# Loading w by row set over all partitions, with two sets of its first quarter in GpSimd's queue

## The chip, the cores and the metric

The kernel runs on one core of one Trainium2 chip. The metric is the device time of one execution in microseconds (us), lower is better. Three runs before the change took 904.36, 904.37 and 904.57 us, median 904.37.

## The reference

x is 16 x 2048 x 1024, w is 1024 x 1024 and decay has 1024 entries, all fp32. The product is followed by a running sum along the sequence that fades by decay at each step:

```
xw = x @ w
out[:, 0] = xw[:, 0]
for t in range(1, S):
    out[:, t] = decay * out[:, t - 1] + xw[:, t]
```

## The kernel before

The 16 x 2048 rows are cut into 64 chunks of 512 rows, and two chunks make a group. A step is one of the eight tiles n (128 columns of w) for one group. TensorE multiplies in bf16 and accumulates over eight tiles k of 128 rows of w. ScalarE (ACT), VectorE (DVE) and GpSimd (POOL) then form the running sum (lines 171 to 254: pairs of neighbours are joined on GpSimd, VectorE scans every second element, GpSimd fills in the others), VectorE transposes the result (line 266), and SP stores it.

x is loaded by `load` (line 105) in GpSimd's queue, cast to bf16 on the way. One load brings a quarter q of x's columns into 32 partitions, for blocks j0 to j1 of 32 rows each. VectorE transposes blocks of 32 x 32 (`turn`, line 115) into `xw`, where two bf16 neighbours stay together as a pair; `part` (line 123) splits the pairs into `xt`. A matmul (line 131) can read either the pairs or `xt`.

The order of all work around the start is written out by hand in `agenda`, letter by letter; `pin` keeps it as the order on each engine and queue. The entry -99 is the start:

```
-99: "M0 U0 M1 M2 M3 U1 U2 w0 W1 w2 W3 K0 K1 K2 K3 E0 E1 G0 E2 G1 E3 F2 G3 W4 w5 W6 W7 D ..."
```

- M0 and M1 are the first and second part of chunk 0, M2 and M3 of chunk 1, four loads each (one for each q). The parts are set by `cuts`: nine and seven blocks for chunk 0, eight and eight for chunk 1.
- w comes in quarters (h, e): h is the half of its columns, e the parity of k. A quarter has four sets m, and k = 2m + e. Quarter (0, 0) is loaded as fp32 in SP's and ACT's queues before the agenda begins, two loads each; U0, U1 and U2 bring (0, 1), (1, 0) and (1, 1) as bf16 in GpSimd's queue. `load_w` (line 307) issues four loads for a quarter, each of them one q in 32 partitions with all four m. The quarters lie in `room`, two output buffers (`ot`) that are not needed yet.
- w0, W1, w2, W3 settle quarter (0, 0): `settle` (line 314) copies one set m into `wsb`, on ScalarE (small letter) or VectorE (capital). W4 to W7 settle (0, 1), W8 to W11 (1, 0), w12 to w15 (1, 1).
- K0 to K3 (line 348) copy one element of each of M0's four loads into a gate; spins, matmuls on zeros (line 332), keep TensorE busy before and behind them.
- E (turn), F and G (part) prepare the parts of chunks 0 and 1, D prepares decay. L loads a quarter of a later chunk.

At step 0 the matmuls of chunks 0 and 1 for n = 0 to 3 run in four parts of 32: chunk 0's first part, even k and then odd k; its second part in the same way; chunk 1's first part; chunk 1's second part. After them step 4 asks for the half h = 1 of w.

GpSimd's loads have eight semaphores in turn. So a load is issued only when the load eight before it in that queue has landed.

Of the kernel before, what the change touches and what calls it, by code (L numbers as in the profile page):

```python
# [10 lines left out]
BF16 = mybir.dt.bfloat16  # L11
# [3 lines left out]
def _ap(ap_obj: bass.AP, new_ap, extra_offset=0):  # L15
    return dataclasses.replace(
        ap_obj,
        ap=[list(p) for p in new_ap],
        offset=ap_obj.offset + extra_offset,
    )  # L20
# [5 lines left out]
def kernel(  # L26
# [26 lines left out]
    nc = tc.nc  # L53
    pin = tc.keep_in_program_order
    B, S, D = x.shape
    assert w.shape == (D, D)

    NQ = 4
    P = 32
    CQ = D // NQ  # L60
    K = CQ // P
    M = K // 2
    TL = 512
    NJ = TL // P
    NC = S // TL
    R = K // 2
    CH = D // 2
# [8 lines left out]
    def ring(pool, name, count, shape, dtype=FP32):  # L76
        i = turns[name] = turns.get(name, -1) + 1
        return pool.tile(shape, dtype, name=f"{name}{i % count}")

    def quad(q):  # L80
        return slice(q * P, (q + 1) * P)
# [12 lines left out]
    def ot_tile(nj):  # L94
        return ring(sb, "ot", 4, [128, nj, CR])
# [3 lines left out]
    xt_of = {}  # L99
# [25 lines left out]
    def matmul(ps, n, k, xt, t0=0, t1=TL, start=0, pairs=None):  # L125
        if pairs is None:
            rhs = xt[:, k // 2, k % 2, t0:t1]
        else:
            rhs = pairs[:, k // 2, t0 // P:t1 // P, :, k % 2].rearrange("p j i -> p (j i)")
        lhs = wsb[:, k, n].rearrange("p q i -> p (q i)")  # L130
        pin(nc.tensor.matmul(  # L131
            out=ps[:, t0:t1] if ps.shape[1] >= t1 else ps,
            lhsT=lhs,
            rhs=rhs,
            start=(k == 0 and t0 == start),
            stop=(k == K - 1),
        ))
# [3 lines left out]
    class Tile:  # L141
# [45 lines left out]
        def copy(self):  # L187
            self.xs = sb.tile([128, 2 * TL], FP32, name=f"xs{self.lot % 3}")[:, 0:self.T]
            size = self.T // len(self.parts())
            for i, ps in enumerate(self.parts()):  # L190
                pin(nc.scalar.copy(out=self.xs[:, i * size:(i + 1) * size], in_=ps))  # L191
# [82 lines left out]
    class Outlet:  # L274
# [8 lines left out]
        def store(self, b, t0):  # L283
# [4 lines left out]
            for j in range(0, self.nj, nj):  # L288
# [8 lines left out]

    room = [ot_tile(2 * NJ).rearrange("p j c -> p (j c)") for _ in range(2)]
    size = M * CH
    stage = {(0, 0): room[0][:, 0:size],  # L300
             (0, 1): room[0][:, size:size * 3 // 2].bitcast(BF16),
             (1, 0): room[1][:, 0:size // 2].bitcast(BF16),
             (1, 1): room[1][:, size // 2:size].bitcast(BF16)}

    def load_w(queues, h, e):
        for i, q in enumerate((0, 2, 1, 3)):
            pin(queues[i % len(queues)].dma_start(  # L307
                out=stage[h, e][quad(q)].rearrange("p (m d) -> p m d", m=M),
                in_=_ap(w, [[2 * D, P], [2 * P * D, M], [1, CH]],
                        (q * CQ + e) * D + h * CH)))  # L310

    def settle(h, e, m, copy):
        src = stage[h, e][:, m * CH:(m + 1) * CH]
        pin(copy(out=wcols[:, 2 * m + e, h],
                 in_=src.rearrange("p (q r i) -> p q r i", q=NQ, r=R)))

    idle = const.tile([128, TL], BF16, name="idle")
    spare = ring(psp, "spare", 1, [128, TL])
    rows = const.tile([128, 2, P], FP32, name="rows")
    touch = const.tile([128, 1], BF16, name="touch")  # L320
    load_w((nc.sync, nc.scalar), 0, 0)
    pin(nc.vector.memset(idle, 0.0))  # L322
    pin(nc.vector.memset(rows, 0.0))
    pin(nc.scalar.copy(out=touch, in_=idle[:, 0:1]))
# [8 lines left out]

    spin(22, idle[:, 0:128])
    H = NJ // 2
    cuts = (((0, H + 1), (H + 1, NJ)), ((0, H), (H, NJ)))
    for q in range(NQ):
        pin(nc.sync.dma_start(
            out=rows[q * P:q * P + R],
            in_=_ap(decay, [[P, R], [CH, 2], [1, P]], q * CR)))  # L340
# [8 lines left out]
        spin(3 if q < NQ - 1 else 1, gates[q])  # L349

    def load_part(i):
        load_w((nc.gpsimd,), *((0, 1), (1, 0), (1, 1))[i])

    def part_one(i, copy):
        part(i // 8, copy, i % 4, i % 4 + 1, *cuts[i // 8][i // 4 % 2])
# [29 lines left out]
    def bank(name, count):  # L385
        return ring(psp, name, count, [128, R, 128])

    def cross(rs, some):
        for i in some:
            for r in rs:  # L390
                t = 2 + i * 128
                pin(nc.tensor.transpose(  # L392
                    out=blocks[i][:, r], in_=tiles[len(slots) - R + r].so[:, t:t + 128], identity=ident))
# [27 lines left out]
    def turn_and_load(c):  # L421
# [38 lines left out]
        "L": lambda i: load(*loads.pop(0)) if loads else None,  # L460
    }
    agenda = {
        -99: "M0 U0 M1 M2 M3 U1 U2 w0 W1 w2 W3 K0 K1 K2 K3 E0 E1 G0 E2 G1 E3 F2 G3 W4 w5 W6 W7 D E4 E5 G4 E6 G5 E7 F6 G7 E8 E9 G8 E10 G9 E11 F10 G11 E12 L E13 G12 L E14 G13 E15 L F14 G15",
        0: "p0 z0 W8 W9 W10 W11",
        1: "g0",
        2: "L S1 L",
# [76 lines left out]
    def rest(s):  # L543
        do = [f"S{s - 1}"] if tiles[s - 1].paired else []
        do.append(f"C{s - 1}")
        if tiles[s - 2].paired:
            do.append(f"B{s - 2}")
        return do + [f"B{s - 1}"] + later.get(s, []) + ["L"] * len(loads)

    def perform(do):  # L550
        for deed in do:
            deeds[deed[0]](int(deed[1:] or 0))
# [3 lines left out]
    for step, (g, n) in enumerate(slots):  # L556
        T = TL * len(g)
        left = step - len(slots)
        if n % R == 0:
            ns, nj = range(n, n + R), T // P  # L560
            if left == -2 * R:
                outlets = [Outlet(ns, H, half) for half in range(2)]
            else:
                pieces = 1 if left < -7 * R else 2 if left < -6 * R else nj // H
                outlets = [Outlet(ns, nj, pieces=pieces)]
        if left == -R:
            outlets = []
        if step == 0:
            heads = [ring(psp, "ps", 3, [128, T]) for _ in range(3)]
            firsts = [ps[:, 0:TL] for ps in heads] + [spares[0]]  # L570
            seconds = [ps[:, TL:T] for ps in heads] + [spares[1]]
            for j0, j1 in cuts[0]:
                for e in range(2):
                    for k in range(e, K, 2):
                        for i in range(R):
                            matmul(firsts[i], i, k, xt_of[0], j0 * P, j1 * P, j0 * P,
                                   pairs=None if e else xw_of[0])
            for k0 in range(0, K, 2):
                for i in range(R):
                    for k in (k0, k0 + 1):  # L580
                        matmul(seconds[i], i, k, xt_of[1], 0, H * P,
                               pairs=xw_of[1] if k0 < 4 else None)
            for i in range(R):
                for k in range(K):
                    matmul(seconds[i], i, k, xt_of[1], H * P, TL, H * P,
                           pairs=xw_of[1] if i < 2 else None)
        if step < R:
            ps = heads[n] if n < 3 else tuple(spares)
        else:
            if step == K + 1:  # L590
                ps = nexts
            elif len(g) == 2 or n % R < 3:
                ps = ring(psp, "ps", 3, [128, T])
            else:
                ps = ring(psp, "spare", 1, [128, TL])
            todo = [(k, l) for k in range(K) for l in range(len(g))]
            if step < K:
                todo.sort(key=lambda kl: kl[0] % 2)
            elif step == K:
                todo = []  # L600
                nexts = (ring(psp, "spare", 1, [128, TL]), ring(psp, "ps", 3, [128, T])[:, TL:T])
                for l in range(len(g)):
                    for i, one in enumerate((ps[:, l * TL:(l + 1) * TL], nexts[l])):
                        for k in range(K):
                            matmul(one, n + i, k, xt_of.get(g[l]),
                                   pairs=xw_of[g[l]] if l or not i and k >= M else None)
            elif step == K + 1:
                todo = []
            if left == -1:
                ps = tuple(both[:, t:t + TL // 2] for t, both in zip(  # L610
                    (0, TL // 2), (ps, ring(psp, "ps", 3, [128, TL]))))
                blocks += [bank("spare1", 1), bank("ps", 3)]
                for t, half in zip((0, TL // 2), ps):
                    for k in range(K):
                        matmul(half, n, k, xt_of[g[0]], t, t + TL // 2, t)
                    if not t:
                        cross((1,), (0, 1))
                todo = []
            for k, l in todo:
                matmul(ps[:, l * TL:(l + 1) * TL], n, k, xt_of[g[l]])  # L620
        tiles.append(Tile(g, n, ps, outlets))
        do = agenda.get(step, agenda.get(left) if left >= -20 else None)
        if do is None:
            do = usual(step)
        else:
            do = do.split()
            if left == -20:
                do = rest(step) + do
        perform(do)
# [29 lines left out]
```

## Time and profile before

| what | value |
|---|---|
| median of three runs | 904.37 us |
| profiled execution | 905.1 us, span 903.3 us |
| TensorE busy | 896.9 us (99%) |
| VectorE busy | 824.2 us (91%) |
| ScalarE busy | 685.9 us (76%) |
| GpSimd busy | 657.1 us (73%) |
| DMA, first 24 us | about 180 to 390 GB/s from 2 us on |

All times in the profile are in us from the start of the span. An idle time stands with the instruction that ends it and with what released that instruction. A load's issue is short; its bytes move later, and it has landed when all the DMA engines that carry it have added to its semaphore. The trace records every packet of the DMA engines with its queue, start and size, and every landing.

### The profile page before, as it was taken

Reading aid. Unit: us, or ns where it says so; the run is one execution under the profiler, and the core shown is the slowest. Engines: PE = TensorE matmul, PEld = TensorE weight load, DVE = VectorE, ACT = ScalarE, POOL = GpSimd, SP = SyncE. Lnnn points to the kernel's source line nnn. Section 1 sums busy time; section 2 is a strip of 40 time slices with the busy share of each in tenths; the row PEclk is TensorE's granted clock in tenths of the full one; section 3 lists DMA queues with packets and bytes.
Section 4 is the critical chain, followed back from the end, with each engine's and each line's share of the span. In section 5 each row is a group of like instructions: output and inputs, shape, how many; then the busy total and the mean of one; then the engine's idle time right before and its main releaser. Section 6 shows DMA issues by size and latency. Waiting matters only on the chain.

```text
span 903.3 us, 12163 instructions
## 1 busy us (share of the span) xinstructions
PE 896.9 (99%) x4216; PEld 412.8 (46%) x4216; DVE 824.2 (91%) x632; ACT 685.9 (76%) x957; POOL 657.1 (73%) x755
## 2 busy tenths in 40 slices
PE   9999999999999999999999999999999999999998
PEld 5444444444444444444444444444444444444444
DVE  4899998998999999999998999999999999999998
ACT  4899867877877877878778778777787787787743
POOL 7978678877767778777677687777777776876632
PEclk9999999999999999999999999999999999999999
DMA  9999999999999999999999999999999999999858
GB/s 193 184 215 215 223 244 208 215 229 232 248 239 251 253 241 246 250 258 249 241 237 226 222 231 226 232 229 227 233 227 226 233 231 222 227 230 214 184 143 232
DMA packets 403182, 204.77 MB, mean 227 GB/s; under 512 B 9392, under 2 KB 402096, under 8 KB 403120
## 3 DMA queue, kind: packets, MB, share of 16 engines
q1 hardware_dynamic: 265808, 134.77, 60.9%
q0 software_dynamic: 137024, 68.70, 56.4%
q8 instruction: 33, 0.54, 0.2%
q10 hardware_dynamic: 288, 0.52, 0.2%
q14 instruction: 29, 0.24, 0.1%
HBM read 138.42 MB, written 134.22 MB: 302 GB/s over the span
## 4 chain that ended last, share of the span: by engine, by line
PE 92%; DMA 3%; DVE 2%; issue 1%; POOL 1%; ACT 0%; DVEq 0%; POOLq 0%; ACTq 0%
PE ps L131 91%; DMA xb<-in_x_dram 2%; POOL xb L105 1%; DMA ot<-in_w_dram 1%; PE spare L131 1%; DVE so L229 1%; DVE ot L266 0%; DVE so L210 0%; DVE xw L115 0%; POOL xs L205 0%; PE spare L392 0%; PE ps L392 0%; ACT h L171 0%; DVE h L401 0%; POOL so L199 0%
## 5 line engine op out<-in xcount | busy, mean ns | idle before, releaser
L131 PE MATMUL ps<-xt,wsb 128*128 128x512 bf16 (+1 forms) x4024 | 865.6, 378 | 0.4 <-DVE so L229 0.4
L131 PEld LDWEIGHTS <-wsb 128*128 128x128 bf16 x4168 | 407.3, 98 | 479.0 <-issue 1.7
L205 POOL TENSOR_TENSOR xs<-h,xs 128x512 f32<-128x512 f32 (+1 forms) x190 | 242.8, 1278 | 183.1 <-ACT h L171 84.6
L266 DVE STREAM_TRANSPOSE ot<-so 128x1024 f32<-128x1024 f32 (+2 forms) x264 | 300.1, 1175 | 5.7 <-DMA out_dram<-ot 3.6
L191 ACT COPY xs<-ps 128x1024 f32<-128x1024 f32 (+1 forms) x190 | 188.8, 994 | 145.2 <-PE ps L131 141.6
L254 POOL TENSOR_TENSOR so<-h,xs 128x512 f32<-128x512 f32 (+1 forms) x190 | 241.1, 1271 | 48.0 <-ACT h L171 28.1
L123 ACT COPY xt<-xw 128x2048 bf16<-128x2048 bf16 (+3 forms) x136 | 242.1, 1788 | 8.9 <-DVE xw L115 8.9
L105 POOL DMA_DIRECT2D xb<-in_x_dram x264 | 174.2, 661 | 6.7 <-DMA xb<-in_x_dram 3.1
L171 ACT ACTIVATE h<-so,dec 128x512 f32<-128x512 f32 (+1 forms) x190 | 145.3, 765 | 37.3 <-DVE so L210 34.0
L115 DVE STREAM_TRANSPOSE xw<-xb 128x2048 f32<-128x2048 f32 (+3 forms) x78 | 147.4, 1902 | 8.8 <-DMA xb<-in_x_dram 8.8
L210 DVE TENSOR_TENSOR_SCAN so<-spare,keep,xs 128x512 f32<-128x512 f32 (+1 forms) x97 | 119.6, 1236 | 24.1 <-POOL xs L205 23.9
L210 DVE TENSOR_TENSOR_SCAN so<-spare,xs 128x512 f32<-128x512 f32 x93 | 113.2, 1219 | 26.4 <-POOL xs L205 23.5
L171 ACT ACTIVATE h<-ps,dec 128x512 f32<-128x512 f32 (+1 forms) x190 | 129.9, 683 | 0.0
L229 DVE TENSOR_TENSOR_SCAN so<-dec,ps 128x1024 f32<-128x1024 f32 x34 | 76.8, 2261 | 1.0 <-ACT h L171 1.0
L229 DVE TENSOR_TENSOR_SCAN so<-dec,keep,ps 128x1024 f32<-128x1024 f32 (+1 forms) x35 | 75.9, 2169 | 0.0
L258 ACT COPY keep<-so 128x1 f32<-128x1 f32 x136 | 25.3, 189 | 9.6 <-DVE so L229 9.0
L201 ACT COPY so<-keep 128x1 f32<-128x1 f32 x97 | 18.4, 191 | 2.7 <-DVE ot L266 2.5
L131 PE MATMUL ps<-xw,wsb 128*128 128x256 bf16 (+3 forms) x72 | 12.3, 306 | 0.4 <-DVE xw L115 0.4
L131 PE MATMUL spare<-xt,wsb 128*128 128x512 bf16 (+3 forms) x60 | 12.6, 330 | 0.0
L199 POOL MEMSET so<- 128x1 f32 x93 | 10.6, 116 | 0.6 <-DVE ot L266 0.6
L332 PE MATMUL spare<-idle 128*128 128x512 bf16 x22 | 7.4, 515 | 1.2 <-DVE idle L322 1.2
L307 POOL DMA_DIRECT2D ot<-in_w_dram x12 | 6.5, 545 | 1.0 <-issue 0.4
(39 smaller groups left out, 37.9 us busy)
## 6 DMA issues: line engine op xcount, KB each, us to landing
out_dram<-ot SPq DMA_DIRECT2D x236, 512.0 KB, 11.1
xb<-in_x_dram POOLq DMA_DIRECT2D x248, 256.0 KB, 7.9
out_dram<-ot SPq DMA_DIRECT2D x56, 128.0 KB, 2.6
out_dram<-ot SPq DMA_DIRECT2D x8, 256.0 KB, 4.0
ot<-in_w_dram POOLq DMA_DIRECT2D x12, 128.0 KB, 6.1
xb<-in_x_dram POOLq DMA_DIRECT2D x8, 128.0 KB, 4.8
out_dram<-xb SPq DMA_DIRECT2D x3, 256.0 KB
xb<-in_x_dram POOLq DMA_DIRECT2D x4, 144.0 KB, 6.2
```

Of the source, the lines that this page charges most:

```text
L105: pin(nc.gpsimd.dma_start(out=xb_of[c][quad(q), j0:j1], in_=_ap(x, [[D, P], [P * D, j1 - j0], [1, CQ]], (b * S + t0 + j0 * P) * D + q * CQ)))
L115: pin(nc.vector.transpose(out=dst.rearrange("p (m j i) -> p j m i", m=M, i=P)[:, j0:j1, m0:m1], in_=src.rearrange("p (j m c) -> p j m c", ...
L123: pin(copy(out=xt_of[c][:, m0:m1, :, j0 * P:j1 * P], in_=src))
L131: pin(nc.tensor.matmul(out=ps[:, t0:t1] if ps.shape[1] >= t1 else ps, lhsT=lhs, rhs=rhs, start=(k == 0 and t0 == start), stop=(k == K - 1),))
L171: pin(nc.scalar.activation(out=h[:, i * size:(i + 1) * size], in_=src, func=mybir.ActivationFunctionType.Copy, scale=dec[:, self.n:self.n ...
L191: pin(nc.scalar.copy(out=self.xs[:, i * size:(i + 1) * size], in_=ps))
L205: pin(nc.gpsimd.tensor_tensor(out=odds, in0=self.g, in1=odds, op=ALU.add))
L210: pin(nc.vector.tensor_tensor_scan(out=so[:, 3:T + 2:2], data0=squares[-1][:, n:n + 1].to_broadcast([128, T // 2]), data1=self.xs[:, 1:T:2 ...
L229: pin(nc.vector.tensor_tensor_scan(out=so[:, t + 2:t + 2 + size], data0=dec[:, n:n + 1].to_broadcast([128, size]), data1=ps, initial=befor ...
L254: pin(nc.gpsimd.tensor_tensor(out=self.so[:, 2:T + 2:2], in0=self.h, in1=self.xs[:, 0:T:2], op=ALU.add))
L258: pin(nc.scalar.copy(out=self.keep, in_=self.so[:, self.T + 1:self.T + 2]))
L266: pin(nc.vector.transpose(out=outlet.ot[:, :, c0:c0 + P], in_=self.so[:, 2 + t0:2 + t0 + nj * P].rearrange("p (i t) -> p i t", t=P)))
```

## The change

A load of w now brings one set m of a quarter for all four q, that is 128 partitions with one row of 512 columns each, instead of one q with four sets. Its source runs over the four quarters q, then 32 rows, then 512 columns. Of quarter (0, 0), set 0 is loaded in SP's queue and set 1 in ACT's, as fp32; sets 2 and 3 come in GpSimd's queue as bf16 and stand there before chunk 0's first part. The units of U are renumbered: U0 is these two sets, U1 to U3 are the other quarters, four loads each. A settle waits for its own set alone. Chunk 0's first part has ten blocks instead of nine, chunk 1's first part seven instead of eight, and the matmuls of chunk 1 take their bound from `cuts`.

```diff
-    stage = {(0, 0): room[0][:, 0:size],
-             (0, 1): room[0][:, size:size * 3 // 2].bitcast(BF16),
+    stage = {(0, 1): room[0][:, size:size * 3 // 2].bitcast(BF16),
...
-    def load_w(queues, h, e):
-        for i, q in enumerate((0, 2, 1, 3)):
-            pin(queues[i % len(queues)].dma_start(
-                out=stage[h, e][quad(q)].rearrange("p (m d) -> p m d", m=M),
-                in_=_ap(w, [[2 * D, P], [2 * P * D, M], [1, CH]],
-                        (q * CQ + e) * D + h * CH)))
+    def spot(h, e, m):
+        if (h, e) == (0, 0):
+            if m < 2:
+                return room[0][:, m * CH:(m + 1) * CH]
+            return room[0][:, 2 * CH:3 * CH].bitcast(BF16)[:, (m - 2) * CH:(m - 1) * CH]
+        return stage[h, e][:, m * CH:(m + 1) * CH]
+
+    def load_w(queue, h, e, m):
+        pin(queue.dma_start(
+            out=spot(h, e, m),
+            in_=_ap(w, [[CQ * D, NQ], [2 * D, P], [1, CH]],
+                    (2 * P * m + e) * D + h * CH)))
...
-    load_w((nc.sync, nc.scalar), 0, 0)
+    load_w(nc.sync, 0, 0, 0)
+    load_w(nc.scalar, 0, 0, 1)
...
-    cuts = (((0, H + 1), (H + 1, NJ)), ((0, H), (H, NJ)))
+    cuts = (((0, H + 2), (H + 2, NJ)), ((0, H - 1), (H - 1, NJ)))
...
     def load_part(i):
-        load_w((nc.gpsimd,), *((0, 1), (1, 0), (1, 1))[i])
+        for m in range(0 if i else 2, M):
+            load_w(nc.gpsimd, i // 2, i % 2, m)
...
-        -99: "M0 U0 M1 M2 M3 U1 U2 w0 W1 w2 W3 ...
+        -99: "U0 M0 U1 M1 M2 M3 U2 U3 w0 W1 w2 W3 ...
...
-                        matmul(seconds[i], i, k, xt_of[1], 0, H * P,
+                        matmul(seconds[i], i, k, xt_of[1], 0, Q,
```

## The prediction

> **What bounds the kernel now.** I read the page first, then the chain of waits for the first 70 us, then the timeline of the first 26 us and around 40 and 68 us, then the trace's packet and landing records of the first 45 us.
>
> The page: TensorE is busy from end to end at full clock, so only its start and its few gaps can be won or lost.
>
> ```profile
> PE 896.9 (99%) x4216; PEld 412.8 (46%) x4216; DVE 824.2 (91%) x632; ACT 685.9 (76%) x957; POOL 657.1 (73%) x755
> PEclk9999999999999999999999999999999999999999
> ```
>
> The chain (start, duration, what) shows that everything up to 68 us hangs on transfers and on who may issue the next one:
>
> ```profile
> 1.31 6.19 DMA xb<-in_x_dram
> ...
> 15.70 6.52 DMA ot<-in_w_dram
> ...
> 28.51 11.19 DMA xb<-in_x_dram
> ...
> 65.62 2.32 DVE so L229
> ...
> 67.98 2.10 PE ps L131 x9
> ```
>
> The timeline (start, duration, engine, line, tile, count, idle time before it and its releaser) has the waits that the change touches:
>
> ```profile
> 6.92 1.14 ACT L314 CAST wsb<-ot 128x512 bf16<-128x512 f32 x2 [3.75 <-DMA ot<-in_w_dram]
> 9.77 1.56 DVE L115 STREAM_TRANSPOSE xw<-xb 128x288 f32<-128x288 f32 x4 [2.05 <-DMA xb<-in_x_dram]
> 10.61 0.55 PE L131 MATMUL ps<-xw,wsb 128*128 128x288 bf16 x3
> 12.45 0.70 DVE L314 COPY wsb<-ot 128x512 bf16<-128x512 bf16 x3 [0.78 <-DMA ot<-in_w_dram]
> 15.31 0.46 PE L131 MATMUL ps<-xw,wsb 128*128 128x224 bf16 x3 [0.38 <-DVE xw L115]
> 22.50 2.03 POOL L105 DMA_DIRECT2D xb<-in_x_dram  x3 [1.53 <-DMA ot<-in_w_dram]
> 39.83 2.31 DVE L115 STREAM_TRANSPOSE xw<-xb 128x2048 f32<-128x2048 f32 x1 [1.38 <-DMA xb<-in_x_dram]
> 67.98 1.24 PE L131 MATMUL ps<-xt,wsb 128*128 128x512 bf16 x5 [0.45 <-DVE so L229]
> ```
>
> To be seen: the first matmul (10.61) waits for chunk 0's first part (last landing 9.64), not for w's first quarter (last landing 6.76). GpSimd's queue is full from 5.2 to 26 us; its loads land one after the other. Its issue of chunk 2 (22.50) waits for the first load of w's third quarter, eight loads earlier (landed 22.22). Chunk 3 lands at 39.70, VectorE takes it at 39.83 and is then busy without a gap, and at 67.98 TensorE waits 0.45 for VectorE. So two things set the end: when TensorE starts, with 0.45 us of slack, and when GpSimd's queue reaches chunk 2, without any.
>
> **The change, part by part.**
>
> Form of w's loads. Before, a load has 32 rows of partitions outermost; after, its source has the four quarters outermost (4, then 32 rows). The only loads of before with four outermost are decay's: each has one landing record at issue and then four more (6.40 to 6.54 for the first), where every other early load has sixteen. So four engines carry such a load in SP's queue, and I take that for the two new ones in SP's and ACT's queues. The Trainium skill, "DMA: Bandwidth & Descriptors", section "Why a DMA increments its semaphore by 16 and not by 1", says that the engine count is the largest number up to 16 that divides the outermost sizes of both sides, and that SP's and ACT's queues use the lowest-numbered engines; it speaks against this change, the trace's decay loads agree in the count, and no run here shows which engines.
>
> Cost of that. Each of the two loads has 128 packets of 2 KB; on four shared engines that is 64 packets each, at 84 ns (their median between 2.2 and 3.8 us) 5.4 us. From the first packet (1.76) this ends at 7.15; decay's 32 small packets behind them on SP's queue, 8 per engine at the 40 ns of the smallest x packets, add about 0.35: 7.5. Spread over all engines it would be 16 packets each, done by 4.0 like the first pair of before, whose end markers ran from 3.3 to 4.0. If the two loads fell on different fours: 32 packets, 4.8.
>
> GpSimd's queue. U0 (two sets, all partitions) now stands ahead of M0. For loads in this queue I know only all sixteen engines. A half-quarter load there takes 0.65 us from landing to landing with 8 packets per engine, 81 ns each; two make 1.3. M0 has 20 packets per engine and load instead of 18, at 40 ns (0.72 per load over 18): four make 3.2. The four slow engines finish M0 at 7.5 + 1.3 + 3.2 = 12.0; with 0.95 from last packet to last landing (before, the late engines ended M0 near 5.6 + 0.2 + 2.9 = 8.7, and it landed at 9.64) M0 lands at 12.9 instead of 9.64. GpSimd issues the first eight loads without a wait, as before, so its two extra issues (0.55 each) lie under this; without that cover they cost 1.1.
>
> TensorE's start. Before: 0.97 after M0's last landing, of which 0.2 was the spins' backlog (the last spin started at 10.39, the transpose was ready at 10.26). After: the spins run dry and wait for the gates, so 0.8 plus the wider transpose (0.04): 13.7.
>
> The four parts, 32 matmuls each. Spacings before: 288 columns 127 and 122 ns (pairs, copies), 224 98, 256 112. Ten blocks (320) 141 and 136: 4.43 us; seven 3.13; nine 4.0. Six (192 columns) have no row: bounded by the 224-column spacing, 98 ns (weight loads take 96 there), 3.1, and by the columns, 84 ns, 2.7. I lean to neither. The Trainium skill, "TensorE: Matmul & The Clock Gate", section "Back-to-back issue gap", has 81 ns sustained for 128 columns, which would make it 2.7; no run here shows it. Sum 14.25 to 14.7 against 14.95 (10.61 to 25.56): settling by set removes the 0.15 at 12.79; and the 0.38 at 15.31 goes, since M1 lands 4.6 after M0 (U1 2.6, four loads of 12 packets per engine 2.0) and is transposed 0.55 later, while the ten blocks end 0.84 + 4.43 = 5.27 after it. Neither stall comes back later: M2 and M3 are ready over half a us before TensorE asks for them. TensorE reaches step 4 at 27.95 to 28.4, that is 2.4 to 2.85 late; at 67.98 that is 69.9 to 70.4.
>
> Chunk 2's issue. On the slow engines after M0 (12.0): U1 2.6, M1 2.0, M2 2.35, M3 3.0 (42 ns, chunk 1's rate), U2's first 0.65: 22.6, landed 23.6 against 22.22, 1.4 late. Before, that load landed 2.07 after its predecessor where its followers took 0.2 to 0.65: one engine was 1.4 late. Is it one of the four, it is 2.8 late. This moves on through chunk 3 and VectorE's gapless work: 69.3 to 70.7.
>
> Settling by set: three waits more on VectorE and on ACT; queued behind are U0's casts, E0 and the G copies, all of which need M0 anyway. Cost nothing while M0 lands last; else up to one copy (0.62). Casting two sets from bf16 instead of fp32 changes nothing there.
>
> Sum: the later of both at 67.98 is 69.9 to 70.7, 1.95 to 2.7 late, middle 2.35. The profiled execution has 905.1 (span 903.3), 0.7 above the median of 904.37; on the median: **906.7**. For this case alone 905.9 to 907.4.
>
> **Rivals.**
>
> *GpSimd's w loads too on four engines each, taken in turn.* For: the same shape. Against: no load in that queue ever showed it. U0's first load then puts 2.6 instead of 1.3 on its four engines; if they are the slow ones, M0 lands 1.3 later still, and since each issue waits for the load eight before, chunk 2's issue moves by 1.3 to 2.9. 908.0 to 909.6, say 908.6.
>
> *Not slower: the loads spread over all engines, and the queue starts earlier.* GpSimd's first packet moved at 5.22, 3.9 us after its issue, just as SP's and ACT's packets ran out; a store of SP's at 38.48 likewise had its first packet at 42.21. So a newcomer waits for what is already queued. With half a MB less ahead, GpSimd's queue starts near 3.45, 1.75 earlier, and has 1.3 more to carry: everything in it is 0.45 earlier from U1 on, chunk 2's issue too. M0 lands at 9.5, the spins still end at 10.61, the parts save 0.25 to 0.7. End 0.45 earlier: 903.9. It decides if the new loads show sixteen landings; two different fours give about 904.3. Against: decay's four landings.
>
> **How the numbers follow.** Forecast 0.50, GpSimd's queue on fours too 0.28, spread 0.20, something else 0.02. 0.2% of 904.37 is 1.8 us, about what a measurement of this kernel can tell from no change: faster is below 902.6, slower above 906.2. Slower: 0.85 of the forecast's chance (its range starts below 906.2), nearly all of the second, together 0.68. Within: most of the rest of both and of the spread case, 0.25. Faster: 0.07, if the spread case also wins the 0.45 at 67.98 and the start. The range takes in the spread case and half of the second, 903.7 to 908.9.
>
> **What would show it.** Right: SP's and ACT's w loads with four landings after the one at issue, landing near 8; M0's last landing near 12.9; first matmul near 13.7, no stall between the parts; chunk 2's first issue between 23.8 and 25.2; TensorE near full afterwards. Wrong: those two loads landed by 5 and GpSimd's first packet near 3.5; or M0 before 10.5; or M0 after 14, which is the second case. A TensorE clock that drops while it waits for M0 between 8.6 and 10.5 would add to any of them.

## The result, and the profile after

The changed kernel takes 916.7 us (four runs, 914.97 to 918.07) against 904.38 beside it on the same chip (904.36 to 904.57): a ratio of 1.0135, 95% interval 1.0117 to 1.0152. The forecast was 906.7, its range ended at 908.9, and the direction was right, but it is 10 us short. The profiled execution of the changed kernel has 916.87 us and a span of 915.1, that is 11.8 more span than before.

The page of the changed kernel (busy time by engine, granted clock in 40 slices, then the queues with packets, MB and share of the DMA engines):

```profile
PE 897.7 (98%) x4216; PEld 412.6 (45%) x4216; DVE 825.2 (90%) x632; ACT 686.0 (75%) x957; POOL 660.1 (72%) x757
PEclk8999999999999999999999999999999999999999
...
q0 software_dynamic: 142688, 68.98, 56.9%
...
q10 hardware_dynamic: 132, 0.26, 0.1%
```

The same two queues on the page of the kernel before:

```profile
q0 software_dynamic: 137024, 68.70, 56.4%
...
q10 hardware_dynamic: 288, 0.52, 0.2%
```

TensorE works as long as before (897.7 against 896.9 us); what is new is idle time. The clock is below full in the first slice alone. q10 is ACT's queue: 132 packets are the 128 rows of its one load and four more, one for each engine that tells of its landing; before, 288 were two loads of 128 and sixteen more for each. So four engines carried the new load. And q0, GpSimd's queue, moves 0.4% more bytes in 5664 more packets: 256 are the rows of the two loads that are new in this queue, 5408 have 4 bytes. Of these 5408, 32 tell of the landings of those two loads, sixteen each; the other 5376 are 384 for each of the 14 loads of w, which fits 32 on each of twelve engines.

The chain of waits of the changed kernel, its start (start, duration, what):

```profile
1.28 12.48 DMA ot<-in_w_dram
...
14.80 6.15 DMA ot<-in_w_dram
...
21.23 2.96 POOL xb L105 x5
...
24.90 10.41 DMA ot<-in_w_dram
```

Before, the chain began with a load of x and named w once, for 6.52 us; now three loads of w in GpSimd's queue take 29 of the first 35 us. The timeline of the changed kernel, at the places shown of before (start, duration, engine, line, tile, count, idle time before it and its releaser):

```profile
12.44 0.62 ACT L318 CAST wsb<-ot 128x512 bf16<-128x512 f32 x1 [9.05 <-DMA ot<-in_w_dram]
15.05 3.62 PE L337 MATMUL spare<-idle,gate 128*128 128x512 bf16 x10 [7.54 <-ACT gate L353]
18.51 0.59 PE L131 MATMUL ps<-xw,wsb 128*128 128x320 bf16 x3
23.56 0.42 PE L131 MATMUL ps<-xw,wsb 128*128 128x192 bf16 x3 [0.45 <-DVE xw L115]
32.56 2.51 PE L131 MATMUL ps<-xw,wsb 128*128 128x288 bf16 x16 [3.02 <-DVE xw L115]
14.05 1.42 POOL L312 DMA_DIRECT2D ot<-in_w_dram  x2 [7.46 <-DMA ot<-in_w_dram]
34.57 0.67 POOL L105 DMA_DIRECT2D xb<-in_x_dram  x1 [1.71 <-DMA ot<-in_w_dram]
51.47 2.31 DVE L115 STREAM_TRANSPOSE xw<-xb 128x2048 f32<-128x2048 f32 x1 [1.14 <-DMA xb<-in_x_dram]
79.61 30.59 PE L131 MATMUL ps<-xt,wsb 128*128 128x512 bf16 x141 [0.18 <-DVE so L229]
```

The first matmul on data comes at 18.51 (before 10.61). GpSimd's ninth load waits 7.46 us, at 14.05, for its first to land. The fourth part of step 0 waits 3.02 us for chunk 1's last blocks (M3). Chunk 2 is issued at 34.57 (22.50). Step 4 begins at 36.87 against 25.56, 11.31 late, which is nearly the whole 11.8. So the loss lies in the first 37 us.

The other path that the prediction followed is as late. Chunk 3 lands at 51.34 (39.70 before), VectorE takes it at 51.47, 11.64 later than before, and the matmul that waited 0.45 for VectorE at 67.98 now waits 0.18 for it at 79.61. So TensorE and VectorE reach this place within 0.2 us of each other, and by these two numbers mending one of the two paths alone would have brought next to nothing.

The landing records say how this came. Twelve of the sixteen landings of GpSimd's first load of w stand at 3.32 to 3.66 us, the other four at 13.21 to 13.76. Its second load has eight by 4.21, four at 7.46 to 8.20, four at 13.81 to 14.51. So I read that each of its loads puts its data on four engines, that the other twelve move only small packets for it, and that all sixteen must post (add to the semaphore). The records name no engine. The first load's four seem to be the ones busy with SP's and ACT's loads: its last landing, at 13.76, comes after that of SP's load (12.42). The next seven loads of the queue have their last four landings at 13.81 to 17.00, that is after those four, however early their other engines were done.

### The profile page after: what moved, and what is told of

Read it like the earlier page. It is cut to its first block, busy times and chain, and to the rows that moved or that the text cites. A ratio compares the mean times of both kernels' runs of the same rounds, so it can differ in the third digit from the quotient of the medians.

```text
span 915.1 us, 12150 instructions
## 1 busy us (share of the span) xinstructions
PE 897.7 (98%) x4216; PEld 412.6 (45%) x4216; DVE 825.2 (90%) x632; ACT 686.0 (75%) x957; POOL 660.1 (72%) x757
## 4 chain that ended last, share of the span: by engine, by line
PE 91%; DMA 5%; POOL 2%; ACT 1%; issue 1%; DVE 0%; POOLq 0%; DVEq 0%; ACTq 0%
PE ps L131 90%; DMA ot<-in_w_dram 3%; DMA xb<-in_x_dram 1%; POOL xb L105 1%; PE spare L131 1%; ACT xt L123 1%; ACT h L171 0%; POOL xs L205 0%; ACT xs L191 0%; DVE so L229 0%; POOL ot L312 0%; POOL so L254 0%; PE spare L398 0%; PE ps L398 0%; DVE h L407 0%
## 5 line engine op out<-in xcount | busy, mean ns | idle before, releaser
L123 ACT COPY xt<-xw 128x2048 bf16<-128x2048 bf16 (+4 forms) x136 | 242.2, 1790 | 13.5 <-DVE xw L115 13.4
L115 DVE STREAM_TRANSPOSE xw<-xb 128x2048 f32<-128x2048 f32 (+4 forms) x78 | 147.4, 1902 | 12.0 <-DMA xb<-in_x_dram 10.2
L312 POOL DMA_DIRECT2D ot<-in_w_dram x14 | 9.7, 693 | 11.7 <-DMA ot<-in_w_dram 7.5
L131 PE MATMUL ps<-xw,wsb 128*128 128x512 bf16 (+4 forms) x72 | 12.6, 307 | 3.5 <-DVE xw L115 3.5
L131 PE MATMUL spare<-xt,wsb 128*128 128x512 bf16 (+5 forms) x60 | 12.6, 330 | 0.0
L318 DVE COPY wsb<-ot 128x512 bf16<-128x512 bf16 x8 | 2.5, 320 | 9.8 <-DMA ot<-in_w_dram 9.8
L199 POOL MEMSET so<- 128x1 f32 x93 | 10.7, 116 | 0.6 <-DVE ot L266 0.6
```

The lines of the kernel that those rows point to most:

```text
L115: pin(nc.vector.transpose(out=dst.rearrange("p (m j i) -> p j m i", m=M, i=P)[:, j0:j1, m0:m1], in_=src.rearrange("p (j m c) -> p j m c", ...
L123: pin(copy(out=xt_of[c][:, m0:m1, :, j0 * P:j1 * P], in_=src))
L131: pin(nc.tensor.matmul(out=ps[:, t0:t1] if ps.shape[1] >= t1 else ps, lhsT=lhs, rhs=rhs, start=(k == 0 and t0 == start), stop=(k == K - 1),))
```

## The experiments

The table has the medians, and from each trace, in us: M0's last landing, the first matmul on data, the last landings of M1 and M3, chunk 2's first issue, the start of step 4. From step 4 to the end of the span ten of the twelve traces have 877.0 to 878.2 us; the two others, marked *, have 2.3 and 1.5 more than before.

| kernel | median us | M0 | first matmul | M1 | M3 | chunk 2 issued | step 4 |
|---|---|---|---|---|---|---|---|
| before | 904.4 | 9.64 | 10.61 | 14.72 | 20.15 | 22.50 | 25.56 |
| before_cuts | 904.79 | 9.93 | 11.08 | 14.51 | 20.19 | 22.19 | 25.32 |
| hw16_sw16_oldcuts | 905.81 | 10.91 | 11.56 | 16.14 | 21.73 | 22.65 | 26.98 |
| hw16_sw16 | 906.21 | 11.27 | 11.96 | 15.90 | 21.86 | 23.36 | 26.82 |
| m0first_k | 906.83 | 9.23 | 10.09 | 15.88 | 22.66 | 24.40 | 27.62 |
| m0first | 907.64 | 8.48 | 14.54 | 15.13 | 21.86 | 22.80 | 28.78 |
| hw4_sw16_spins | 910.06 | 13.60 | 14.41 | 18.64 | 25.86 | 26.68 | 30.82 |
| hw4_sw16 | 910.70 | 13.75 | 15.97 | 18.29 | 25.11 | 26.03 | 30.22 |
| hw16_sw4 * | 912.38 | 13.87 | 14.56 | 18.26 | 25.78 | 29.36 | 30.74 |
| cursor | 914.89 | 15.97 | 16.66 | 21.03 | 29.74 | 32.19 | 35.85 |
| spins * | 916.44 | 16.76 | 19.10 | 22.94 | 29.92 | 33.10 | 34.88 |
| the change | 916.7 | 16.61 | 18.51 | 23.00 | 31.91 | 34.57 | 36.87 |

Names: hw is SP's and ACT's loads of w, sw GpSimd's; 4 is the changed form (four q outermost), 16 that of before. In the form of before a load brings one q, so U0 is four loads instead of two, and SP and ACT have two loads each instead of one.

**hw16_sw16: all of the change but the form of the loads.**

```diff
...
+    def load_q(queues, h, e, m0, m1):
+        for i, q in enumerate((0, 2, 1, 3)):
+            pin(queues[i % len(queues)].dma_start(
+                out=part_of(h, e, m0, m1)[quad(q)].rearrange("p (m d) -> p m d", m=m1 - m0),
+                in_=_ap(w, [[2 * D, P], [2 * P * D, m1 - m0], [1, CH]],
+                        (q * CQ + 2 * P * m0 + e) * D + h * CH)))
...
-    load_w(nc.sync, 0, 0, 0)
-    load_w(nc.scalar, 0, 0, 1)
+    load_q((nc.sync, nc.scalar), 0, 0, 0, 2)
...
-        for m in range(0 if i else 2, M):
-            load_w(nc.gpsimd, i // 2, i % 2, m)
+        load_q((nc.gpsimd,), i // 2, i % 2, 0 if i else 2, M)
```

(`part_of`, not shown, gives the place of sets m0 to m1.)

> The change's order, split (half of the first quarter on SyncE and ScalarE, half on GpSimd) and cuts, but every w load as in the kernel before: one q on 32 partitions, with all its sets, so that the source's outermost dimension has 32 entries. Theory A (the four-entry outermost dimension puts each load's data on four engines, and this alone is the loss): M0 lands at about 9 us (16.6 in the changed kernel, 9.64 before), chunk 2 is issued by about 22.5 (34.57), the stall of 3.0 us before the fourth part is gone, and the time is 903.5 to 904.8. Theory B (the order of the loads, or the cuts, cost by themselves): 906 or more, with stalls before the second and fourth parts.

906.21 us, ratio 1.002 (1.0011 to 1.0029). Its timeline, and a line of its queues:

```profile
1.31 2.29 POOL L326 DMA_DIRECT2D ot<-in_w_dram  x4 [0.86 <-POOLq L662]
3.58 2.36 POOL L105 DMA_DIRECT2D xb<-in_x_dram  x4
...
11.39 1.69 DVE L115 STREAM_TRANSPOSE xw<-xb 128x320 f32<-128x320 f32 x4 [3.11 <-DMA xb<-in_x_dram]
```

```profile
q0 software_dynamic: 137344, 68.96, 56.8%
```

10.5 of the 12.3 us are gone with the form, and so are the small packets of q0; no stall is left between the parts. But neither theory holds whole: M0 lands at 11.27, not at 9, and 1.7 us of loss stay, without the stalls that theory B named. Those belong to the split of the first quarter, its order, or the cuts.

**hw4_sw16 and hw16_sw4: the form in one of the two queues.** Each takes one of the two replacements of the diff above: hw4_sw16 the second (GpSimd's), hw16_sw4 the first.

> Only GpSimd's w loads get the form of before (one q on 32 partitions, outermost 32); the two loads of SyncE and ScalarE keep four entries outermost. This is the case that the forecast of 906.7 took the changed kernel to be. Theory A (both queues' loads sit on four engines, GpSimd's share of it is what was missed): SyncE's load is still slow, M0 lands at 12 to 13.5, the sixteen-engine loads of GpSimd still wait for the four slow engines, the time is 906 to 908.5. If only the first quarter's placing on four engines made the loss (GpSimd's form is harmless): 914 or more, as in the changed kernel.

> The other half of the pair: the two loads of SyncE and ScalarE come in the form of before (one q on 32 partitions, two sets, outermost 32), GpSimd's w loads stay by row set over all partitions (outermost 4). Theory A (each queue's four-engine loads cost by themselves, and GpSimd's the more since every later load of its queue must pass the four busy engines): M0 lands at 11 to 14, U1 later than 15, chunk 2 is issued at 28 or later, the time is 908 to 913. If SyncE's and ScalarE's slow loads alone had made the loss: as with all loads in the form of before, about 906.2.

hw4_sw16: 910.70 us, 1.0066 (1.0052 to 1.008); hw16_sw4: 912.38, 1.0087 (1.0072 to 1.0103). From the TensorE timelines, hw4_sw16 first, then hw16_sw4:

```profile
12.41 3.73 PE L351 MATMUL spare<-idle,gate 128*128 128x512 bf16 x10 [4.42 <-ACT gate L367]
```

```profile
26.43 2.51 PE L131 MATMUL ps<-xw,wsb 128*128 128x288 bf16 x16 [1.46 <-DVE xw L115]
34.12 12.52 PE L131 MATMUL ps<-xt,wsb 128*128 128x512 bf16 x56 [1.49 <-ACT wsb L332]
```

On top of hw16_sw16 the form costs 4.5 us in SP's and ACT's queues and 6.2 in GpSimd's; together 10.7, and the change has 10.5. So the two add. hw4_sw16 is the case that the forecast of 906.7 describes, and it takes 4.0 more than that; I expected at most 908.5 here too. hw16_sw4 came out as its theory A said. In hw4_sw16 each of GpSimd's first four loads has twelve landings by 5.26, 5.75, 6.12 and 6.61, and four at 7.14 to 9.82: on the shared engines its packets take turns with SP's and ACT's from the start. In hw16_sw4 nothing blocks four engines, yet M0 lands as late, and the late quarters of w bring a wait of their own after step 4 (34.12, for w's last settling). There GpSimd's first load has twelve landings by 5.49 and four, with its data, at 6.45 to 6.63. My reading is that rows of w on four engines at a time leave the engines at different places, and as loads need all sixteen and issues need the load eight before, the queue waits for the last one each time.

**cursor: U0's first load one group of four engines further.**

```diff
-        pin(nc.sync.dma_start(
+        pin((nc.sync if q else nc.gpsimd).dma_start(
             out=rows[q * P:q * P + R],
```

> The changed kernel with the first of the four decay loads moved from SyncE's queue to the head of GpSimd's, so that each later four-engine load of that queue starts its count one group of four engines further on. Theory A (U0's first set landed at 13.76 since its data lay on the same four engines as SyncE's and ScalarE's loads): that collision goes, U0's data is moved by 9; the landings of the whole queue still wait for the four slow engines, so M0 moves by 0 to 4 us and the time is 912 to 917. Rival (the collision with U0 is no part of the loss): within 0.7 of the changed kernel.

914.89 us, 1.0114 (1.01 to 1.0128), against 916.7 for the change. U0's two loads land at 9.79 and 10.20 instead of 13.76 and 14.51: that fits groups which go round in turn, by load, and is what theory A said. M0 gains only 0.64; its last load has twelve landings by 14.69 and the last four at 15.65 to 15.97. But the ninth load is issued at 7.17 instead of 14.05, and M3 lands 2.17 earlier. The median falls by 1.8, nearer to what M3 gained than to what M0 did; in the two traces 1.02 of it is there when step 4 begins and 0.92 comes after. The edit does more than turn the groups: it takes a load out of SP's queue, and the load that it puts at the head of GpSimd's lands at 6.88, which lets the ninth go early. How much each of these is worth, this run doesn't separate. Its TensorE timeline has the start and the stall:

```profile
12.34 3.59 PE L337 MATMUL spare<-idle,gate 128*128 128x512 bf16 x9 [3.74 <-ACT gate L353]
...
30.40 3.66 PE L131 MATMUL ps<-xw,wsb 128*128 128x288 bf16 x16 [2.83 <-DVE xw L115]
```

**spins and hw4_sw16_spins: is it TensorE's start, and its clock?**

```diff
-    spin(22, idle[:, 0:128])
+    spin(60, idle[:, 0:128])
```

> The changed kernel with 60 instead of 22 matmuls on zeros ahead of the gated ones, so that TensorE works on until M0 is near instead of idling for 7.5 us. Theory A (the granted clock of 0.5 makes the gated matmuls and the first part late): the gated ten take 2.3 instead of 3.6 us, the first matmul on data comes 0.7 to 1.2 earlier, and 0 to 1.0 of it reaches the end, since the later stall of 3.0 us (chunk 1's last blocks) waits for data and takes what was won before it: 915.5 to 916.7. Rival (what is won at the start is kept): 915.5 or less.

916.44 us, 1.0133 (1.0119 to 1.0147). Its TensorE timeline:

```profile
16.94 2.32 PE L337 MATMUL spare<-idle,gate 128*128 128x512 bf16 x10
...
30.57 2.51 PE L131 MATMUL ps<-xw,wsb 128*128 128x288 bf16 x16 [1.05 <-DVE xw L115]
37.38 12.53 PE L131 MATMUL ps<-xt,wsb 128*128 128x512 bf16 x56 [0.61 <-ACT wsb L318]
```

The gated ten take 2.32 instead of 3.62 us, so the clock's price is right; but 60 was too many, and the first matmul on data came 0.59 later, not 0.7 to 1.2 earlier. The run still tells what I wanted to know. M3 landed 1.99 earlier in this execution, with the same loads, and step 4 began 1.99 earlier, although the start was later: the stall before the fourth part took up both and fell from 3.02 to 1.05. So on TensorE's own path in the changed kernel the start is not what counts; the landing of M3 and then of w's late quarters (37.38) is.

The same in hw4_sw16, with 38 spins, where no stall came after the start:

> As the run in which only SyncE's and ScalarE's loads keep four entries outermost, with 38 instead of 22 matmuls on zeros ahead of the gated ones. That run had no stall after the first matmul on data, at 15.97, and its gated ten took 3.73 us at a clock of 0.5 after 4.4 us of idle time. Theory (start of TensorE sets the end there, and the clock costs 1.4 of it): the gated ten take 2.3, the first matmul on data comes 1.0 to 1.5 earlier, and the time falls by as much, to 909.2 to 909.9. Rival (a later wait sets the end, as in the changed kernel, where more such matmuls brought nothing): 910.3 to 911.2.

910.06 us (909.68 to 910.93), against 910.70 (909.13 to 911.56): between the two expectations. Its TensorE timeline:

```profile
12.24 2.33 PE L351 MATMUL spare<-idle,gate 128*128 128x512 bf16 x10
...
26.52 2.51 PE L131 MATMUL ps<-xw,wsb 128*128 128x288 bf16 x16 [1.33 <-DVE xw L115]
```

The start is 1.56 earlier, and the fourth part then waits 1.33 for M3. The clock was worth what it should be, and little or none of it reaches the end, as M3's landing lies right behind it: in the two traces step 4 even begins 0.60 later (30.82 against 30.22). Part of that wait is one engine: M3's last load has fifteen landings by 24.31 and the sixteenth at 25.86. Shortly before, at 23.42, stands a packet of 16 KB of the instruction queue (q8) that took 0.95 us; that it is the cause is read from the times alone.

**before_cuts and hw16_sw16_oldcuts: the cuts.** In both the line is the same, set and undone:

```diff
-    cuts = (((0, H + 1), (H + 1, NJ)), ((0, H), (H, NJ)))
+    cuts = (((0, H + 2), (H + 2, NJ)), ((0, H - 1), (H - 1, NJ)))
```

> The kernel before with the cuts at ten and seven blocks and nothing else of the change. Theory A: both small stalls (0.15 before the second part, 0.38 before the fourth) go or shrink, the first part is 0.44 longer and starts when its tenth block is there; 903.9 to 904.6, within 0.1% of before. Theory B (cuts cost): 905.3 or more.

> As the run with every w load in the form of before, and the cuts at nine and eight blocks again. Theory A: the cuts are worth what the stalls before the second and the fourth part cost (0.15 and 0.38 us in the kernel before), less what M0 brings forward; 0 to 0.6 us slower than with ten and seven, and under 905.2. Theory B (ten and seven blocks cost by themselves): faster than with ten and seven.

before_cuts: 904.79 us, 1.0004 (0.9995 to 1.0013), between the two theories, and no difference that can be told. Its first part starts at 11.08, 0.47 later, and nothing stalls until step 4, which starts 0.24 earlier. hw16_sw16_oldcuts: 905.81, 1.0016 (1.0007 to 1.0025); it is 0.4 under hw16_sw16 where theory A had it slower, and their runs overlap (905.55 to 906.75 and 905.49 to 906.83), so theory B is not shown either. The cuts move the stalls, and any effect on the time is within the scatter. Its TensorE timeline:

```profile
14.23 0.54 PE L131 MATMUL ps<-xt,wsb 128*128 128x288 bf16 x3 [0.47 <-DVE wsb L332]
...
16.73 0.46 PE L131 MATMUL ps<-xw,wsb 128*128 128x224 bf16 x3 [0.37 <-DVE xw L115]
```

So with the form of before and nine blocks both old stalls are there, 0.47 (for U1, inside the first part) and 0.37.

**m0first and m0first_k: where the last 1.4 us are.** hw16_sw16 with M0 ahead of U0 (the first letters of the line below); in m0first_k also the gates and the turning of M0 ahead of the settling of U0's two sets (the rest of it).

```diff
-        -99: "U0 M0 U1 M1 ... w0 W1 w2 W3 K0 K1 K2 K3 E0 E1 G0 E2 G1 E3 F2 G3 W4 ...
+        -99: "M0 U0 U1 M1 ... w0 W1 K0 K1 K2 K3 E0 E1 E2 E3 w2 W3 G0 G1 F2 G3 W4 ...
```

> All w loads in the form of before, the change's split and cuts, but chunk 0's first ten blocks ahead of the two w sets in GpSimd's queue. Theory A1 (GpSimd's queue gains nothing from starting 1.7 us earlier, because its loads are moved as they are issued, with several engines idle at times between 5 and 9 us): M0 and U0 both land by 10.5 to 11.3, and the time is 905.5 to 906.5. Theory A2 (it was U0 ahead of M0 that made M0 late): M0 lands at 8 to 9, the first matmul on data at 10 to 11, and the time is 904 to 905.

907.64 us, 1.0034 (1.0022 to 1.0045). Its timeline, ScalarE and then TensorE:

```profile
9.92 0.62 ACT L332 COPY wsb<-ot 128x512 bf16<-128x512 bf16 x1 [4.17 <-DMA ot<-in_w_dram]
10.44 0.83 ACT L366 COPY gate<-xb 32x1 bf16<-32x1 bf16 x4
```

```profile
10.68 4.02 PE L350 MATMUL spare<-idle,gate 128*128 128x512 bf16 x10 [3.24 <-ACT gate L366]
```

M0 lands at 8.48, 2.79 earlier than in hw16_sw16 and 1.45 earlier than in before_cuts. U0's data takes 1.34 of that (8.48 to 9.82). So GpSimd's queue does gain from a shorter SP and ACT load, and it was U0 ahead of M0 that lost it: GpSimd needs 2.27 us for U0's four issues (1.31 to 3.58 above), and M0's loads land 4.3 to 5.2 us after their issue even when they stand first. But the gates stand behind U0's settling on ScalarE, four of them ready at once at 10.44, and TensorE had idled 3.24 us and ran at half clock. So A2 was right about M0 and wrong about the time.

> As the run with chunk 0's first blocks ahead of the two w sets, but the gates of TensorE's warm-up matmuls, and DVE's turning of chunk 0's first blocks, are issued ahead of the settling of those two sets. Theory (in that run M0 was there at 8.5, and the 3 us lost came from the gates, queued on ScalarE behind a settling that waits for a later load, and from the clock of 0.5 after the idle time that followed): the gates follow M0's landings from 5.6 on, the clock stays 1.0, the first matmul on data comes at 9.2 to 10.5 (14.54 there), and a stall of 0.5 to 1.5 us for U1 (landed at 12.4 there) and one of up to 0.7 for M1 (15.1) take back most of it: 903.8 to 905.3. Rival (M0 itself, or something else in that order, is late): 906.5 or more.

906.83 us, 1.0027 (1.0018 to 1.0036). Its TensorE timeline:

```profile
7.93 2.32 PE L350 MATMUL spare<-idle,gate 128*128 128x512 bf16 x10
...
14.35 0.58 PE L131 MATMUL ps<-xt,wsb 128*128 128x320 bf16 x3 [1.70 <-DVE wsb L332]
...
20.20 0.76 PE L131 MATMUL ps<-xw,wsb 128*128 128x224 bf16 x6 [0.80 <-DVE xw L115]
```

The gates are mended, and the first matmul on data comes at 10.09, earlier than in any other kernel here. It brings 0.8 us over m0first and nothing over hw16_sw16: a stall of 1.70 for U1 and one of 0.80 for M2 take more than it gained, and the time is in the rival's range. U1's four loads are now the ninth to twelfth of the queue instead of the fifth to eighth. Before, they were issued from 3.85 to 5.47 without a wait; here each waits for one of M0's to land, from 6.57 to 9.52, and the last lands at 13.82 against 12.33. I read that as the price of giving GpSimd's queue four more loads at its head; no run has the split with fewer loads. With the split, the four kernels without four-engine loads have 905.8 to 907.6 us; without it, and with the new cuts, 904.8. No version here beats the kernel before.

## Why the prediction failed, step by step

- **The failed step** is "For loads in this queue I know only all sixteen engines", under GpSimd's queue. All fourteen loads of w there have data on four engines. The form in that queue costs 6.0 to 6.2 us (916.7 against 910.7; 912.4 against 906.2), which the forecast had at nothing. I weighed it as a rival at 0.28, on the shape alone, and priced it at 908.0 to 909.6: it moved M0 by 1.3 later still and chunk 2's issue by 1.3 to 2.9. Measured, against hw4_sw16, M0 is 2.86 later and chunk 2's issue 8.5. M0 at 16.61 is also the prediction's own sign for this rival (M0 after 14). What the rival missed is that a load's twelve other engines also have to post, and that each late landing holds up the issue eight loads on, again and again (7.46, then waits of 0.84, 0.86, 2.73 and 1.71 us on GpSimd). The Trainium skill, "DMA: Bandwidth & Descriptors", section "Why a DMA increments its semaphore by 16 and not by 1", states that the rule by outermost sizes holds for GpSimd's queue too, which takes the engines in a round from a cursor, and that there all sixteen post whatever the shape. The traces agree: sixteen landings for each of these loads, 384 packets of 4 bytes that fit twelve engines without data, and U0 moved from 13.76 to 9.79 in cursor. I had cited the page for SP and ACT only.
- **SP's and ACT's loads on four shared engines** was right in the count: 132 packets in ACT's queue, one landing record at issue and four later. The landing "near 8" held for ACT's load (6.98, in hw4_sw16 7.40) and not for SP's (12.42 and 10.87). The sum let SP's packets flow from 1.76; in the change the first of them starts at 3.94 and the last at 11.22, in hw4_sw16 at 4.23 and 9.87.
- **The matmuls of the four parts** were right: ten blocks 4.44 us (4.43 said), six 2.70 (2.7 to 3.1 said, no lean), seven 3.12 (3.13). The 192-column spacing is 84 to 85 ns: the bound by columns. That fits the 81 ns for 128 columns that the prediction took from the Trainium skill, "TensorE: Matmul & The Clock Gate", section "Back-to-back issue gap"; no run here shows the 81 itself.
- **The sum of the forecast's own case** was 4.0 short, as hw4_sw16 shows at 910.7. In the profiled executions it was 1.65 short (spans 907.3 and 903.3, 4.0 apart, where 2.35 was forecast); the rest is that the profiled execution of hw4_sw16 was its fastest run, 1.6 under its median, and that of before was 0.7 above its own. What the slower runs of hw4_sw16 lost on top, no trace shows. Two terms: M0 landed at 13.75, not 12.9, and on the way there the packets of GpSimd and SP took turns instead of SP's going first (GpSimd's first four loads had landed by 9.82, SP's one at 10.87); and the first matmul came 2.2 after M0, not 0.8. I named the falling clock as something that "would add" and left it out of the sum: the ten gated spins took 3.73 instead of 2.3, 1.4 us. Together they put the first matmul at 15.97 instead of 13.7. Chunk 2's first issue, the other term, came at 26.03 where 23.8 to 25.2 was said.
- **"Neither stall comes back later"** held for hw4_sw16 and failed for the change: 0.45 before the second part and 3.02 before the fourth, where M3 landed at 31.91. I had taken M2 and M3 as half a us early.
- **Two things set the end**, TensorE's start and GpSimd's queue reaching chunk 2, held in its form: at 79.61 TensorE still waits for VectorE, which is 11.64 late with chunk 3, and TensorE itself is late by nearly as much. But TensorE is not late by its start alone (7.90); the rest are the stalls for M1 and M3, and so GpSimd's queue is behind both paths. In spins the start moved by 0.59 without effect; in cursor M3 moved by 2.17 and the time by 1.8.
- **The rival on the other side**, all loads spread and GpSimd's queue starting earlier, had 903.9. hw16_sw16 comes closest to that case, with U0 in four loads where the rival had two: 906.2. The queue did start near 3.5, as it said, but M0 landed at 11.27 and not at 9.5: U0's 1.3 us of data were counted, the 2.27 us of issues ahead of M0 were not, nor that with four loads U1 loses its place among the first eight.
- **Settling by set costs nothing** held in the change, where M0 lands last. m0first shows the other case: the gates queued behind it, 3.24 us of idle TensorE.

What stays open: how much of GpSimd's 6 us is the uneven place of its engines and how much the small packets (9 ns each) themselves; no run separates them. No run has the change's row sets spread over sixteen engines, so the 10.5 us between the change and hw16_sw16 contain, beside the four engines, whatever else the two forms differ in, such as the number and the size of the loads. That the queue of hw16_sw16 runs dry between U0 and M0 is read from issue times and packets (58 and 38 packets per half us from 5 to 6, where the kernel before, once its queue moves, has 157 and 187 from 5.5 to 6.5), not tested by itself.

## What to carry to other kernels

Before merging loads, look at the outermost dimension of both sides of the new one: here 4 instead of 32 put each load on a quarter of the engines, in every queue, and the late quarter held back loads that had nothing to do with it. In a queue with a fixed number of loads in flight, count a load's place and its issue time, not only its bytes: four more loads at the front took 2.27 us to issue where their data took 1.3 to move. An earlier start of the main engine is worth only what the next late transfer leaves of it; find that transfer before pricing the start.

## What the runs showed that I had not expected

- A load of w in the changed form, in GpSimd's queue, has 384 packets of 4 bytes, which fits 32 on each of the twelve engines without data. They take 9 ns each (median), and these engines post their landing too, some of them within 2.1 us of the issue.
- A load of x in GpSimd's queue with nothing ahead of it in that queue landed 4.3 us after its issue (m0first: issued at 1.32, landed at 5.63, while SP's and ACT's loads landed by 4.97).
- The first 16 KB packet of the instruction queue, at 20 to 28 us in these traces, comes with one late engine, though no run moved it alone: in the changed kernel it came at 28.39, and M3's last load then has its last three landings at 29.58, 30.44 and 31.91. Before, it came at 20.20, just after M3 (20.15), and the loads of w behind M3 have their last landing 0.9 to 1.4 us after the fifteenth (22.22 against 20.78 for the first).
- The granted clock fell to 0.5 while TensorE waited, in steps of 3.41 us: 6.83 us in the change, 3.41 in hw4_sw16 and m0first. cursor had it a second time, in the fourth part, after the stall of 2.83. The windows of the changed kernel (stretch; busy time of TensorE, its weight loads, VectorE, ScalarE, GpSimd; clock; DMA share, which adds up the packets' times and passes 1 where they overlap; GB/s):

```profile
8.00:12.00 4.00, 0.00 (x0) 0.00 (x0) 0.00 (x0) 0.00 (x0) 0.00 (x0) 0.86 1.52 166
12.00:16.00 4.00, 0.95 (x3) 0.40 (x4) 0.29 (x1) 1.62 (x4) 1.87 (x3) 0.50 0.81 84
16.00:20.00 4.00, 4.00 (x20) 1.97 (x19) 2.60 (x7) 2.88 (x6) 3.16 (x7) 0.79 0.75 98
```

From 12 to 20 us the DMA engines move 84 and 98 GB/s, about half of the 166 from 8 to 12: the queue that everything waits for runs nearly empty, because its issue is held up until 14.05.
